# Two 64-row products per pair, padded with zeros to 128 rows

## The chip, the cores and the metric

The kernel runs on one core of one Trainium2 chip. The metric is device time in microseconds (us), as the median of several runs. The core's engines run side by side, each through its own instruction stream in order: TensorE (PE; its weight loads are listed as PEld) does matrix products into PSUM, VectorE (DVE), ScalarE (ACT) and GpSimd (POOL) do elementwise work, and SyncE (SP) issues DMAs, as ScalarE does for the weights.

## The reference

The model is a trunk of two layers over 1024 positions of width 1024, each followed by a SwiGLU block. Layer 0 mixes by spatial gating and pooling. Layer 1 is an RWKV-7 time mix, and of that this part matters here:

```python
wlog = -jax.nn.softplus(-(w0 + jnp.tanh(xw @ w1) @ w2).astype(f32)) - 0.5
...
a = jax.nn.sigmoid(a0 + (xa @ a1) @ a2)
g = jax.nn.sigmoid(xg @ g1) @ g2
...
k = k * (1 + (a - 1) * k_a)
...
decay = heads(jnp.exp(-jnp.exp(wlog)))
y = wkv7_scan(rh, decay, kh, vh, -kk, kk * ah)
```

The decay and the learning rate `a` each come from a product of rank 64: first 1024 to 64 (`w1`, `a1`), then 64 to 1024 (`w2`, `a2`). The gate has rank 160.

## The kernel before

Everything is held transposed, 128 features on the partitions and positions along the free dimension, in two halves of 512 positions. Products are made precise by splitting each float32 operand into a rounded part (hi) and the rest (lo) and adding three products: hi by hi, hi by lo, lo by hi (`mm3`, lines 343 to 346). Weights come by DMA in tiles of 128x1024 (`load_at`, line 108), and are split by ScalarE (line 145) and DVE (line 146) just ahead of their use.

For the two low-rank products of decay and learning rate the rank is 64, and the kernel uses the other 64 partitions for the lo part of the weights. The tiles `w2[0]` and `w2[1]` hold 128 rows: one half has the hi part of the 64 weight rows, the other half the lo part (`stack`, line 148; for decay the lo part is in rows 64 to 127, for the learning rate in rows 0 to 63). In `lowrank` (line 824) the tiles `tw` and `ta` get the hi part of the inner vectors twice, in both halves (line 840), so that one product of 128 rows gives hi by hi and lo by hi at once. The lo parts of the inner vectors share one tile, `twlo`: that of decay in rows 0 to 63, that of the learning rate in rows 64 to 127 (line 842). They meet only the hi half of the weights, in a second product of 64 rows:

```python
for z, w, x, r in ((zw, w2[0], twa[0], rows[0]), (za, w2[1], twa[1], rows[1])):
    pe.matmul(z, w[:, ms], x, start=True, stop=False)
    pe.matmul(z, w[r, ms], twlo[r], start=False, stop=True)
```

This stands at lines 998 to 1000 of `project`, which runs once for each half. Its order is: the gate's second product for 8 blocks of 128 features (lines 919 to 927; it reads the tiles `ghi`, `glo` and the 96-row `gst`, is evicted by ScalarE and sent to memory); then masks set by GpSimd (lines 932 to 937); then a loop over 8 pairs of heads. A pair does the k product (24 matmuls), the four low-rank matmuls above, tanh and sigmoid of their results (lines 1004 to 1007), the running sum of the decay (line 1011), its exponentials (lines 1015 and 1016), the r product (24 matmuls, with small products in between), the norms (lines 1024 to 1027 and 1037), and products of these elementwise (lines 1043 to 1060). The interaction of a pair (`interact`, line 941, with products at line 946) is emitted one pair later. After pairs 3 and 7 its results go through memory into the input of a triangular inversion (`invert`, lines 1106 to 1128), whose 31 steps run on DVE beside the pairs that follow. After the pairs comes the v product (line 1089).

The tiles `ghi`, `tw`, `ta` and `twlo` come from the pool `kp`, with one buffer for each tag.

Except where it is written out by hand, the order of instructions on each engine is made by a planner: it simulates the engines with estimated durations and picks by priority, which is mostly the order in which the program was written, among what it takes to be ready. A tile that takes over a buffer waits for all readers of the tile that had it.

Of the kernel before, what the change touches and what calls it, by code (L numbers as in the profile page):

```python
# [9 lines left out]
F32 = mybir.dt.float32  # L10
F32R = mybir.dt.float32r
AF = mybir.ActivationFunctionType
# [4 lines left out]
P = 128  # L17
# [3 lines left out]
HT = 512  # L21
# [17 lines left out]
def tile_trunk(  # L39
# [8 lines left out]
    act, dve, pool, pe, sp = nc.scalar, nc.vector, nc.gpsimd, nc.tensor, nc.sync  # L48
    x = x.flatten_outer_dims()
# [19 lines left out]
    def open_pool(**kw):  # L69
        es = ExitStack()  # L70
        pl = es.enter_context(tc.tile_pool(reuse_waits="tile", **kw))
        return pl if kw["name"].startswith("wp") else Lines(pl), es
# [60 lines left out]
    def take(key):  # L133
        i = pos[0]
        assert plan[i][0] == key, (plan[i][0], key)
        pos[0] += 1
        split_at(i)
        load_at(i + 1)
        if i + 1 in raws:
            load_at(i + 2)  # L140
        split_at(i + 1)
        return ready.pop(i)
# [189 lines left out]
    def auxt():  # L332
        return pst("aux")
# [234 lines left out]
    for m in ORD_Z:  # L568
# [4 lines left out]
        for h in range(2):  # L573
# [15 lines left out]
            s, w, base = zp, 1, 0  # L589
            while w < win:  # L590
# [4 lines left out]
                s, base, w = n, b0, 2 * w  # L595
# [193 lines left out]
    rows = [slice(0, 64), slice(64, 128)]  # L789
# [110 lines left out]
    def project(h, hn1, kp, ring, keep, before_v):  # L900
# [3 lines left out]
        def tmp(tag, bufs=1, shape=None, dt=F32):  # L904
            if early.get(tag):
                return early[tag].pop(0)
            return ep.tile(shape or [P, HT], dt, tag=tag, bufs=bufs, name=tag)
# [7 lines left out]
        w2 = tmp("w2", 1, [P, D], F32R), tmp("a2", 1, [P, D], F32R)  # L915
# [3 lines left out]
        for m in range(KT):  # L919
            ms = slice(m * P, (m + 1) * P)  # L920
# [6 lines left out]
                sp.dma_start(g_d[h][rows[m % 2], m // 2 * 2 + r, :], t[rows[r]])  # L927
        for n in range(2):
            take(("wa2", n, h))
        twa, twlo = (keep["tw"], keep["ta"]), keep["twlo"]  # L930
        smask = tmp("smask", 1, [P, 256])
        pool.memset(smask, 1.0)
        pool.memset(c64(smask)[:, :, 0:1], 0.0)
# [51 lines left out]
        for p in range(KT):  # L985
            ms = slice(p * P, (p + 1) * P)
# [8 lines left out]
            act.activation(kt, o, AF.Copy)  # L995

            zw, za = auxt(), auxt()
            for z, w, x, r in ((zw, w2[0], twa[0], rows[0]), (za, w2[1], twa[1], rows[1])):
                pe.matmul(z, w[:, ms], x, start=True, stop=False)
                pe.matmul(z, w[r, ms], twlo[r], start=False, stop=True)  # L1000
            if prev is not None:
                late(*prev)
            sg, av = tmp("sg", 2), tmp("av", 2)
# [31 lines left out]
            for j in range(4):  # L1035
                for r in range(2):
                    pe.matmul(
                        rb[rows[r], j * P : (j + 1) * P], bc(rn[:, 2 * j + r : 2 * j + r + 1], [P, 64]), ident,
                        start=True, stop=True,
# [457 lines left out]
    kp, kp_es = open_pool(name="keep0", bufs=1, side="right")  # L1497
    ring, ring_es = open_pool(name="ring0", bufs=1, side="right")
    f, f_es = open_pool(name="ffn0b", bufs=1, side="right")
    parts, keep = project_gate(0, hn1, kp, xlp, ring)  # L1500
# [14 lines left out]
    nxt = {}  # L1515
    ps_es = open_psum("psp0", PROJ)
    project(0, hn1, kp, ring, keep, early("n0", "act1", xlp_es))
    for e in (ring_es, kp_es, np_es):
        e.close()
# [15 lines left out]
    kp, kp_es = open_pool(name="keep1", bufs=1, side="right")  # L1535
# [6 lines left out]
    parts, keep = project_gate(1, hn1, kp, nxt["a"], ring)  # L1542
# [19 lines left out]
    for e in (f_es, y_es, hb_es, ps_es):  # L1562
        e.close()
    ps_es = open_psum("psp1", PROJ)
    project(1, hn1, kp, ring, keep, early("n1", "act2", nxt["a_es"]))
    for e in (ring_es, kp_es, np_es):
        e.close()
# [56 lines left out]
```

## Time and profile before

| | |
|---|---|
| median of 3 runs | 2528.8 us (2524.71 to 2532.28) |
| profiled execution | 2522.66 us, span 2520.9 us |
| mean granted TensorE clock | 0.983 |
| idle time of TensorE at line 1000 | 9.5 us over 32 matmuls, put down to issue |
| DVE lines 1117 and 1122, the inversion | from 825.7 us (first half) |
| SBUF-to-memory and weight traffic | 310.69 MB, mean 123 GB/s |

In the rows of the profile "L1000" is a line of the kernel, "aux<-twlo,w" is output and inputs by the program's names, "64\*128 64x512" is a stationary operand of 64 rows by 128 columns and a moving one of 64 rows by 512, and an arrow at the end names what ended the idle time before. The listed ends of matmuls are modelled and overlap; their starts are what to read.

### The profile page before, as it was taken

Reading aid. Unit: us, or ns where it says so; the run is one execution under the profiler, and the core shown is the slowest. Engines: PE = TensorE matmul, PEld = TensorE weight load, DVE = VectorE, ACT = ScalarE, POOL = GpSimd, SP = SyncE. Lnnn points to the kernel's source line nnn. Section 1 sums busy time; section 2 is a strip of 40 time slices with the busy share of each in tenths; the row PEclk is TensorE's granted clock in tenths of the full one; section 3 lists DMA queues with packets and bytes.
Section 4 is the critical chain, followed back from the end, with each engine's and each line's share of the span. In section 5 each row is a group of like instructions: output and inputs, shape, how many; then the busy total and the mean of one; then the engine's idle time right before and its main releaser. Section 6 shows DMA issues by size and latency. Waiting matters only on the chain.

```text
span 2520.9 us, 37945 instructions
## 1 busy us (share of the span) xinstructions
PE 2432.2 (96%) x15735; PEld 1983.2 (79%) x15735; DVE 1401.8 (56%) x2118; ACT 890.7 (35%) x1335; POOL 299.8 (12%) x298
## 2 busy tenths in 40 slices
PE   8999999999989998999999989899999999999998
PEld 6888888888767786788877667787888878888887
DVE  5445634444865873555457855964654445434443
ACT  6233322222544432333234643433333224323223
POOL 0200000000323410111001222401211000100001
PEclk9999999999999998999999999999999999999999
DMA  5113433323255478433334355585653332423331
GB/s 175 48 59 92 142 109 116 101 92 112 88 156 134 123 204 203 136 113 102 112 118 138 111 179 133 132 230 159 167 150 110 100 107 77 150 88 119 94 92 59
DMA packets 434956, 310.69 MB, mean 123 GB/s; under 512 B 93216, under 2 KB 395424, under 8 KB 433760
## 3 DMA queue, kind: packets, MB, share of 16 engines
q10 hardware_dynamic: 297280, 210.53, 27.9%
q1 hardware_dynamic: 137504, 97.75, 13.7%
q8 instruction: 123, 2.02, 0.3%
q14 instruction: 49, 0.40, 0.0%
HBM read 254.68 MB, written 53.54 MB: 122 GB/s over the span
## 4 chain that ended last, share of the span: by engine, by line
PE 74%; DVE 13%; DMA 7%; issue 3%; ACT 2%; POOL 1%; SPq 0%; ACTq 0%; DVEq 0%; POOLq 0%
PE mm L344 21%; PE mm L345 21%; PE mm L346 20%; PE sm L1168 4%; DVE wlo L146 2%; DMA raw<-in_ffn_w_up_dram 2%; DVE it L1117 1%; DVE mix L887 1%; DVE xi L1122 1%; DMA iat<-at_d 1%; PE yp L1168 1%; DMA raw<-in_ffn_w_down_dram 1%; PE mm L510 1%; PE mm L511 1%; ACT whi L145 1%
## 5 line engine op out<-in xcount | busy, mean ns | idle before, releaser
L344 PE MATMUL mm<-ahi,whi 128*128 128x512 f32 x1952 | 766.9, 394 | 5.1 <-DVE h L423 4.0
L345 PE MATMUL mm<-alo,whi 128*128 128x512 f32 x1952 | 769.1, 394 | 1.6 <-DVE alo L146 1.6
L346 PE MATMUL mm<-ahi,wlo 128*128 128x512 f32 x1952 | 766.5, 393 | 2.6 <-DVE wlo L146 2.6
L145 ACT ACTIVATE whi<-raw 128x1024 fp32r<-128x1024 f32 x288 | 304.3, 1058 | 768.1 <-PE mm L345 608.5
L146 DVE TENSOR_TENSOR wlo<-raw,whi 128x1024 fp32r<-128x1024 f32 x288 | 362.0, 1257 | 309.8 <-ACT whi L145 301.5
L344 PEld LDWEIGHTS mm<-ahi,whi 128*128 128x128 f32 x1952 | 367.9, 189 | 87.2 <-issue 4.5
L346 PEld LDWEIGHTS mm<-ahi,wlo 128*128 128x128 f32 x1952 | 368.2, 189 | 82.3 <-DVE wlo L146 3.4
L345 PEld LDWEIGHTS mm<-alo,whi 128*128 128x128 f32 x1952 | 368.2, 189 | 82.1 <-issue 3.7
L345 PE MATMUL mm<-hidlo,wdhi 128*128 128x512 f32 x624 | 246.6, 395 | 1.3 <-DVE hidlo L672 1.2
L344 PE MATMUL mm<-hidhi,wdhi 128*128 128x512 f32 x624 | 239.8, 394 | 6.6 <-ACT hidhi L671 5.2
L346 PE MATMUL mm<-hidhi,wdlo 128*128 128x512 f32 x624 | 245.5, 393 | 0.0
L423 DVE TENSOR_TENSOR h<-h,mm 128x512 f32<-128x512 f32 x192 | 129.2, 684 | 149.9 <-PE mm L346 149.1
L145 ACT ACTIVATE wdhi<-raw 128x1024 fp32r<-128x1024 f32 x82 | 86.6, 1059 | 254.9 <-DMA raw<-in_ffn_w_down_dram 150.8
L146 DVE TENSOR_TENSOR wdlo<-raw,wdhi 128x1024 fp32r<-128x1024 f32 x82 | 100.4, 1225 | 111.3 <-ACT wdhi L145 105.5
L668 DVE TENSOR_TENSOR sg<-sg,mm 128x512 f32<-128x512 f32 x88 | 60.2, 685 | 165.3 <-PE mm L346 164.9
L344 PEld LDWEIGHTS mm<-hidhi,wdhi 128*128 128x128 f32 x624 | 117.2, 188 | 35.2 <-ACT hidhi L671 7.4
L345 PEld LDWEIGHTS mm<-hidlo,wdhi 128*128 128x128 f32 x624 | 118.2, 189 | 27.9 <-DVE hidlo L672 3.2
L346 PEld LDWEIGHTS mm<-hidhi,wdlo 128*128 128x128 f32 x624 | 118.2, 189 | 24.6 <-issue 0.2
L423 DVE TENSOR_TENSOR hA<-hA,mm 128x512 f32<-128x512 f32 x72 | 48.7, 685 | 77.0 <-PE mm L346 77.0
L349 POOL TENSOR_TENSOR nrs<-nrs,small 128x4 f32<-128x4 f32 x8 | 10.0, 1246 | 625.4 <-DVE nrs L371 625.4
L344 PE MATMUL mm<-xhi,whi 128*128 128x512 f32 (+1 forms) x160 | 66.0, 412 | 4.2 <-ACT k L925 4.2
L672 DVE TENSOR_TENSOR hidlo<-sg,hidhi 128x512 fp32r<-128x512 f32 x88 | 64.5, 733 | 3.8 <-ACT hidhi L671 3.7
(300 smaller groups left out, 2952.1 us busy)
## 6 DMA issues: line engine op xcount, KB each, us to landing
raw<-in_ffn_w_gate_dram ACTq DMA_DIRECT2D x88, 512.0 KB
raw<-in_ffn_w_up_dram ACTq DMA_DIRECT2D x88, 512.0 KB
raw<-in_ffn_w_down_dram ACTq DMA_DIRECT2D x88, 512.0 KB
raw<-in_ab_w_in_dram ACTq DMA_DIRECT2D x16, 512.0 KB
raw<-in_ab_w_out_dram ACTq DMA_DIRECT2D x16, 512.0 KB
raw<-in_rwkv_w_k_dram ACTq DMA_DIRECT2D x16, 512.0 KB
raw<-in_rwkv_w_r_dram ACTq DMA_DIRECT2D x16, 512.0 KB
ar_d<-ar SPq DMA_DIRECT2D x16, 512.0 KB
```

Source lines behind the costliest of these rows:

```text
L145: act.activation(hi, src, AF.Copy)
L146: (eng or dve).tensor_tensor(out=lo, in0=src, in1=hi.bitcast(F32), op=ALU.subtract)
L344: pe.matmul(o, whi, xhi, start=first, stop=False)
L345: pe.matmul(o, whi, xlo, start=False, stop=False)
L346: pe.matmul(o, wlo, xhi, start=False, stop=last)
L423: dve.tensor_tensor(out=H[h][:, m, :], in0=H[h][:, m, :], in1=o, op=ALU.add)
L510: pe.matmul(ops[j], xhi[:, k, sl], whi[:, kk], start=(k == 0), stop=False)
L511: pe.matmul(ops[j], xhi[:, k, sl], wlo[:, kk], start=False, stop=False)
L668: dve.tensor_tensor(out=s, in0=s, in1=o, op=ALU.mult)
L672: dve.tensor_tensor(out=lo, in0=s, in1=hi.bitcast(F32), op=ALU.subtract)
L887: dve.scalar_tensor_tensor(out=t, in0=hn1[:, k, 0:HT], scalar=col(c), in1=t, op0=ALU.mult, op1=ALU.add)
L1168: i = f(*args, **kw)
```

## The change

The tile `twlo` keeps the lo part of decay in rows 0 to 63 and gets zeros in rows 64 to 127. A new tile, `talo`, takes over the buffer of `ghi`; ScalarE copies the lo part of the learning rate into its rows 64 to 127, and GpSimd sets its rows 0 to 63 to zero. The second product of each pair is then made over all 128 rows, with the full weight tile. The zero rows of the moving operand meet the lo half of the weights, so the result is the same.

```diff
         for n in range(2):
             take(("wa2", n, h))
-        twa, twlo = (keep["tw"], keep["ta"]), keep["twlo"]
+
+        twlo, talo = keep["twlo"], kp.tile([P, HT], F32R, tag="ghi", name="talo")
+        act.activation(talo[rows[1]], twlo[rows[1]].bitcast(F32), AF.Copy)
+        pool.memset(talo[rows[0]].bitcast(F32), 0.0)
+        pool.memset(twlo[rows[1]].bitcast(F32), 0.0)
+        twa, low = (keep["tw"], keep["ta"]), (twlo, talo)
...
             zw, za = auxt(), auxt()
-            for z, w, x, r in ((zw, w2[0], twa[0], rows[0]), (za, w2[1], twa[1], rows[1])):
+            for z, w, x, xl in ((zw, w2[0], twa[0], low[0]), (za, w2[1], twa[1], low[1])):
                 pe.matmul(z, w[:, ms], x, start=True, stop=False)
-                pe.matmul(z, w[r, ms], twlo[r], start=False, stop=True)
+                pe.matmul(z, w[:, ms], xl, start=False, stop=True)
```

## The prediction

> **What bounds the kernel now.** I read the page first, then TensorE's timeline around the products that the change touches, then the busy time by stage, and last the waits.
>
> ```profile
> span 2520.9 us, 37945 instructions
> ...
> PE 2432.2 (96%) x15735; PEld 1983.2 (79%) x15735; DVE 1401.8 (56%) x2118; ACT 890.7 (35%) x1335; POOL 299.8 (12%) x298
> ...
> PE 74%; DVE 13%; DMA 7%; issue 3%; ACT 2%; POOL 1%; SPq 0%; ACTq 0%; DVEq 0%; POOLq 0%
> ```
>
> TensorE is busy for 96% of the span and carries 74% of the chain that ended last. Time taken out of its stream is worth something wherever no other engine holds the next step. The stream must be read by starts, though: durations of matmuls overlap, so what one of them really costs is the distance from its start to the start of the next. The edit touches lines 999 and 1000. This is the timeline of TensorE around pair 3 of the first half (start, duration, engine, line):
>
> ```profile
> 790.63 0.39 PE L999 MATMUL aux<-tw,w 128*128 128x512 f32 x1
> 790.95 0.50 PE L1000 MATMUL aux<-twlo,w 64*128 64x512 f32 x1
> 791.38 0.49 PE L999 MATMUL aux<-ta,a 128*128 128x512 f32 x1
> 791.80 0.49 PE L1000 MATMUL aux<-twlo,a 64*128 64x512 f32 x1
> 792.23 0.50 PE L344 MATMUL mm<-ahi,whi 128*128 128x512 f32 x1
> 792.57 0.40 PE L345 MATMUL mm<-alo,whi 128*128 128x512 f32 x1
> 792.81 0.40 PE L346 MATMUL mm<-ahi,wlo 128*128 128x512 f32 x1
> ```
>
> Outside the block a product with 512 columns takes 0.24 us from start to start (792.57 to 792.81), or 0.23 in the rows further down. Inside it the distances are 0.32, 0.43, 0.42, 0.43 and 0.34 us. So five matmuls, the last of which is an ordinary one, take 792.57 - 790.63 = 1.94 us, where five at 0.23 us would take 1.15. The surplus is 0.79 us for a pair, or 0.40 us for each of its two 64-row products, split between the way in and the way out. The last pair of the second half looks the same:
>
> ```profile
> 1603.09 0.39 PE L999 MATMUL aux<-tw,w 128*128 128x512 f32 x1
> ...
> 1605.03 0.40 PE L345 MATMUL mm<-alo,whi 128*128 128x512 f32 x1
> ```
>
> Again 1605.03 - 1603.09 = 1.94 us. The view of the tile twlo (durations in ns as least/median/most) shows that these products are few and alike:
>
> ```profile
> L1000 PE MATMUL aux<-twlo,w x16: 497/498/792, 726.8 to 1603.4; 64*128 64x512 f32 x16
> L1000 PEld LDWEIGHTS aux<-twlo,a x16: 182/183/183, 732.0 to 1604.3; 64*128 64x128 f32 x16
> L1000 PE MATMUL aux<-twlo,a x16: 491/491/498, 732.0 to 1604.3; 64*128 64x512 f32 x16
> ```
>
> There are 32 of them, two for each of 8 pairs in each of 2 halves. At 0.40 us each the whole surplus is 12.8 us, or 0.5% of the span. That is the ceiling of the direct gain.
>
> **Is it the 64 rows?** The timeline holds a product with a third number of rows, the 96-row one of the gate:
>
> ```profile
> 731.24 0.39 PE L346 MATMUL mm<-ghi,wlo 128*128 128x512 f32 x1
> 731.47 0.40 PE L923 MATMUL mm<-gst,whi 96*128 96x512 f32 x1
> 731.70 0.40 PE L999 MATMUL aux<-ta,a 128*128 128x512 f32 x1
> ```
>
> It fits into the stream at 0.23 us on either side, although it too has fewer rows than the products around it, another stationary operand, and closes an accumulation of its own. So neither a smaller count of rows by itself nor the close of a group costs anything here; going from the 128-row form to the 64-row form and back does. A product padded to 128 rows has the shape of its neighbours, and I take its cost to be theirs, 0.23 us. The Trainium skill, page "TensorEngine Tiling (Array Packing)", section "Key Properties", has a rule that would give this sum: a change of the tiling mode drains the array. Its page "TensorE: Matmul & The Clock Gate", section "Why this matters for your kernels", has one that speaks against the change: a single product of 32 rows takes the same time as one of 128, so rows would be free and zeros would buy nothing. The rows above (0.43 against 0.23 us) agree with the first; the second comes back as a rival.
>
> **What passes to the end.** The pairs do not all lie under the same bound. Busy time in two stretches of each half (start:end and length, then PE, PEld, DVE, ACT, POOL, then the granted clock):
>
> ```profile
> 757.00:824.00 67.00, 67.00 (x474) 52.60 (x474) 35.67 (x48) 26.68 (x39) 22.24 (x24) 1.00 0.55 141
> 824.00:880.00 56.00, 50.87 (x333) 39.08 (x331) 52.29 (x95) 26.71 (x40) 26.18 (x21) 0.94 0.44 111
> 1499.00:1564.00 65.00, 65.00 (x453) 51.23 (x454) 34.69 (x47) 25.98 (x38) 22.21 (x24) 1.00 0.57 146
> 1564.00:1622.00 58.00, 52.45 (x342) 40.95 (x342) 53.15 (x96) 26.68 (x40) 26.33 (x21) 0.94 0.42 108
> ```
>
> In the first stretch of each half, pairs 1 to 4, TensorE never idles and the clock is 1.00, with DVE at 35.67 of 67 us. There each 0.79 us passes in full: 8 pairs x 0.79 = 6.3 us.
>
> In the second stretch, pairs 5 to 7, DVE is busy for 52.29 of 56 us, because the inversion (lines 1117 and 1122) has joined it, and TensorE is the one that waits:
>
> ```profile
> PE aux L946 <- DVE bk L1055: 7.4, 5, 3.4
> PE aux L999 <- DVE w L153: 6.5, 2, 4.6
> ...
> PE mm L344 <- ACT k L925: 4.2, 2, 2.1
> ```
>
> The stretch begins when the inversion gets its input after a round trip by DMA, for which DVE stands idle:
>
> ```profile
> 825.69 0.19 DVE L1117 TENSOR_TENSOR it<-iat,xi 128x31 f32<-128x31 f32 x1 [6.49 <-DMA iat<-at_d]
> ```
>
> That input comes from pair 3's interaction product, which follows the block of pair 4, so it comes forward by what pairs 1 to 4 save. What pairs 5 to 7 save themselves may only make the waits on DVE longer. Their 6 pairs x 0.79 = 4.7 us are worth between 0 and 4.7 us. DVE at 93% (52.29 of 56) speaks for little, TensorE at 91% (50.87 of 56) for much; I take half, 2.4 us.
>
> **What is added.** For each half: one ScalarE copy of 64x512, and two GpSimd fills of 64x512. The nearest rows, of the view of line 840 and of the groups by form:
>
> ```profile
> L840 ACT ACTIVATE tw<-low x4: 613/623/632, 667.2 to 1408.8; 64x512 fp32r<-64x512 f32 x4
> ```
>
> ```profile
> L1142 POOL MEMSET state_d<- 128x512 f32 x1 | 0.5, 524 | 0.0
> ```
>
> The copy is 0.62 us and a fill 0.52 us, by the row with as many columns, so 0.62 us of ScalarE and 1.05 us of GpSimd in each half, on engines busy for 35% and 12%. The padded product reads the full 128x128 weight tile, which the product before it loads anyway; the weights need no new instruction.
>
> More important is an ordering. The new tile takes the single buffer of ghi, so the copy has to wait for the last gate product that reads ghi. The copy reads the rows of twlo that are then set to zero, so both low products of pair 0 wait for this chain, that of decay too. In the trace of before they ran early, at 726.80 and 732.03, as filler between gate products. Queued behind the copy on ScalarE are evictions, splits and the tanh of pair 0; behind the fills on GpSimd stand smask, ind2 and the inversion's first fill. These rows tell who would notice:
>
> ```profile
> 734.18 0.39 PE L923 MATMUL mm<-gst,whi 96*128 96x512 f32 x1
> ...
> 736.67 0.50 PE L344 MATMUL mm<-xhi,whi 128*128 128x512 f32 x1 [2.10 <-ACT k L925]
> ...
> 738.43 0.64 ACT L1015 ACTIVATE epx<-cum 128x512 f32<-128x512 f32 x1
> ...
> 749.50 0.69 DVE L1059 TENSOR_TENSOR ar<-mm,epx 128x512 f32<-128x512 f32 x1 [3.35 <-DMA raw<-in_rwkv_w_k_dram]
> ```
>
> The gate ends at 734.18 + 0.39 = 734.57; a copy and one fill later (1.14 us) it is 735.7, and TensorE now waits for ScalarE until 736.67. That 2.10 us of idle time covers the chain; were it gone, the chain would cost 1.1 us a half. Pair 0's exp at 738.43 has 11.1 us until its first use at 749.50, so a later sigmoid and scan are covered as well. The bounds for pair 0, both halves together: a gain of about 3 us, half of the 6.5 us for which TensorE waits for DVE w at its first product, if that one no longer stands ahead of the gate's (half, because no row tells how soon the gate's could start), and a loss of about 4 us, if 1.1 us of chain and 0.9 us of displaced filler (four products at 0.23) stand open in each half. The idle row lies nearest to nothing lost, so I take 0, and also for its own share of the surplus (32 - 28 = 4 products, 1.6 us), since it sits in a stretch where TensorE waits anyway.
>
> **The sum.** 6.3 + 2.4 + 0 = 8.7 us less. The profiled execution took 2522.66 us, of which 2520.9 are its span; by the sum the same execution would take 2514.0 us. It lies 6.1 us below the median of the runs, 2528.8; applied to the median, the forecast is 2520.1 us.
>
> **Rivals.** *The gain is given back on other engines.* The products get cheaper, but pairs 5 to 7 pass nothing on (2.4 us less gain) and pair 0 pays its 4 us: 6.3 - 4 = 2.3 us gained, 2526.5 us. For it speak DVE's 93% and the in-order wait of ScalarE just where the copy goes in; against it the 2.10 us of idle cover. The planner orders all instructions by its own estimate of when each is ready, and three more instructions a half can shift that order; this too falls in here.
>
> *Rows are free.* The surplus of 0.79 us belongs to something that padding doesn't touch, so nothing is saved, and the copy's 0.62 us stands open in each half: 2528.8 + 1.2 = 2530.0 us. This is also the case in which the change does not do what it says. For it stands that part of the surplus, the 0.32 us from 790.63 to 790.95, already follows a 128-row product; against it the 96-row product, which has everything but the 64-row form and costs 0.23 us. The Trainium skill's rule on a single small product, named above, would give this case; the trace bears it out badly.
>
> *Pair 0 comes late.* The planner, seeing that the low products of pair 0 must wait, may put them behind its k product and its r product, 24 matmuls each, 11 us together. Then they come not at 726.80 but at about 736.67 + 11.0 = 747.7, 20.9 us later, and the exp follows by as much: past the 11.1 us of slack by about 10 us, for which DVE would stand at line 1059 with the splits of the next weights queued behind it. Open in both halves, that is 20 us against 8.7 gained: 2540 us. It turns the result to the slow side from 8.2 us a half on ((8.7 + 7.6) / 2). Against it: the low product needs only the copy and a fill, and TensorE is idle at just that time.
>
> **How the numbers follow.** A measurement of this kernel can tell about 0.3%, 7.6 us, from no change. The forecast with its mechanism has 0.57, given back 0.30, rows free 0.05, pair 0 late 0.08. Faster by over 0.3% means below 2521.2; the forecast lies only 1.1 us beyond that line, so the chances are 0.57 faster, 0.35 the same (given back and rows free), 0.08 slower. The range starts at the ceiling with pair 0's gain, 2528.8 - 12.8 - 3 = 2513.0, and ends at 2529.0, just past no change; the late pair and the worst of rows free stay outside.
>
> **What would show it right or wrong.** The products of lines 999 and 1000 should both read 128x512, 16 for each operand, and stand 0.23 us apart, so that the block from the first to the second matmul behind it takes about 1.15 us instead of 1.94; if it still takes 1.9, rows are free. The stretch of pairs 1 to 4 should be shorter by about 3 us in each half, with TensorE still without idle time. In pairs 5 to 7 the wait on DVE bk should grow by less than 2.4 us a half; if by all of that, I put too much there. At the end of the gate, the wait for ScalarE should not exceed 2.1 us and no wait for GpSimd should appear on the first low product; if one of several us does, pair 0 was mispriced. Waits in the recurrence and in the dense stages should be as before; if they differ by several us, the order was laid anew and my sum is not the whole story.

## The result, and the profile after

The changed kernel takes 2514.06 us (median of 7 runs, 2508.43 to 2517.13), beside 2525.61 us for the kernel before in the same series (7 runs, 2522.41 to 2532.28). The ratio, which goes by the means of the runs, is 0.9947, with a 95% interval of 0.9933 to 0.9962: 13.4 us less, give or take 3.7. The two medians lie 11.6 us apart. The forecast was 8.7 us less, and 2520.1 us as a time; that time started from a median of 3 runs, 2528.8 us, which lies 3.2 us above the one of 7. The profiled execution took 2514.61 us, with a span of 2512.9 us.

The first thing to read is the block that the change touches. This is the changed kernel's TensorE timeline around pair 3 of the first half (start, duration); lines 999 and 1000 are now 1004 and 1005:

```profile
787.23 0.39 PE L1004 MATMUL aux<-tw,w 128*128 128x512 f32 x1
787.45 0.39 PE L1005 MATMUL aux<-twlo,w 128*128 128x512 f32 x1
787.68 0.39 PE L1004 MATMUL aux<-ta,a 128*128 128x512 f32 x1
787.91 0.39 PE L1005 MATMUL aux<-talo,a 128*128 128x512 f32 x1
788.13 0.39 PE L344 MATMUL mm<-ahi,whi 128*128 128x512 f32 x1
788.36 0.39 PE L345 MATMUL mm<-alo,whi 128*128 128x512 f32 x1
```

All starts are 0.22 or 0.23 us apart, and from the first matmul to the second one behind the block it is 788.36 - 787.23 = 1.13 us, where it was 1.94. The change does what it says, at a price per product that is the neighbours' own.

Next, the stages. The table is worked out from starts of matmuls in the two profiled executions. "Pair 0" runs from the third 96-row product of the gate to pair 1's first low-rank product; "pairs 1 to 4" from there to pair 5's; "pairs 5 to 7" from there to the last interaction product of pair 7; the other rows lie between these.

| stage, us | before | after | difference |
|---|---|---|---|
| pair 0, first half | 37.99 | 35.13 | -2.86 |
| pairs 1 to 4 | 65.34 | 62.53 | -2.81 |
| pairs 5 to 7 | 66.25 | 65.41 | -0.84 |
| between the halves | 573.3 | 570.0 | -3.3 |
| pair 0, second half | 34.95 | 32.37 | -2.58 |
| pairs 1 to 4 | 65.34 | 62.77 | -2.57 |
| pairs 5 to 7 | 66.64 | 67.74 | +1.10 |
| tail: from there to the last matmul | 881.6 | 887.1 | +5.5 |

One execution of each is not enough to trust single rows, so both were profiled again, as they are and with one small fill written twice (experiment 1), and the 96-row kernel of experiment 2, whose order is that of the changed one, counts with it. Averaged over three profiles on the side of the kernel before and four on that of the changed one, pair 0 gained 2.9 and 1.6 us, pairs 1 to 4 2.8 and 2.6, pairs 5 to 7 0.4 and then lost 0.9, the stretch between the halves gained 3.4, and the tail lost 3.9. Pairs 1 to 4 hardly vary (65.34 each time before, 62.52 to 62.85 after). Pair 0 of the second half does (32.37 to 35.69 after), and so does the tail: 881.6 to 886.7 before, 886.9 to 891.2 after.

Pairs 1 to 4 by engine (start:end and length, then busy us of PE, PEld, DVE, ACT, POOL, then the granted clock, the share of the DMA engines' time and GB/s), the kernel before and then the changed kernel, two halves each:

```profile
759.10:824.40 65.30, 65.30 (x456) 51.48 (x455) 34.69 (x47) 26.03 (x40) 22.24 (x24) 1.00 0.57 145
1498.90:1564.30 65.40, 65.40 (x457) 51.50 (x455) 34.69 (x47) 26.14 (x40) 22.21 (x24) 1.00 0.57 145
```

```profile
756.80:819.30 62.50, 62.01 (x457) 51.76 (x456) 34.70 (x47) 25.74 (x40) 22.23 (x24) 1.00 0.59 152
1487.10:1549.90 62.80, 62.07 (x457) 51.81 (x456) 34.70 (x47) 25.79 (x40) 22.23 (x24) 1.00 0.59 151
```

The same work on every engine, in less time; but PE is now idle for 0.5 and 0.7 us, where it had no idle time. The wait view of the first of these stretches names what is late next:

```profile
PE aux L1042 <- POOL rn L349: 0.5, 1, 0.5
```

That is one wait in pair 1 for the norms that GpSimd works on. From pair 2 on, the distance from pair to pair (first low-rank product to first low-rank product) is 16.03 us, before 16.89.

Pairs 5 to 7, before (the first two rows) and after:

```profile
824.40:890.70 66.30, 61.17 (x393) 47.51 (x391) 62.02 (x111) 29.62 (x44) 30.02 (x24) 0.90 0.48 128
1564.30:1630.90 66.60, 57.67 (x391) 45.19 (x391) 61.55 (x109) 29.55 (x44) 30.62 (x24) 0.95 0.47 125
```

```profile
819.30:884.70 65.40, 57.42 (x392) 46.70 (x391) 61.16 (x109) 29.36 (x44) 30.02 (x24) 0.92 0.48 127
1549.90:1617.60 67.70, 55.98 (x393) 46.44 (x391) 61.40 (x110) 29.31 (x44) 28.58 (x24) 0.93 0.47 125
```

DVE is busy for 62 us of 66 before and for 61 us of 65 to 68 after. PE's busy time falls by 3.8 and 1.7 us, and the stretch by 0.8 us in the first half, while it grows by 1.1 in the second. The granted clock moves the same way, up in the first half and down in the second. The waits of the changed kernel (over the whole span: total us, times, longest) that answer to those shown of before read:

```profile
PE aux L951 <- DVE bk L1060: 14.3, 6, 3.6
PE sm L1173 <- DVE gt L1220: 8.8, 3, 3.9
...
PE aux L1004 <- DVE w L153: 5.8, 2, 4.0
...
PE sm L1175 <- DMA bk<-bk_d: 4.1, 2, 3.4
...
PE aux L1005 <- ACT talo L932: 2.8, 2, 1.4
```

Of the kernel before, the two that the prediction does not show are:

```profile
PE sm L1168 <- DVE gt L1215: 10.8, 6, 4.1
...
PE sm L1170 <- DMA bk<-bk_d: 1.9, 1, 1.9
```

The wait for DVE bk grew from 7.4 to 14.3 us. Within pairs 5 to 7, over the three and four profiles, it grew by 1.8 us in the first half and 5.0 in the second. The idle time before the k product (4.2 us, twice 2.1) is gone from the list, and a wait of 1.4 us a half on the copy `talo` has come.

Last, pair 0. The changed kernel's timeline at the end of the gate:

```profile
733.39 0.39 PE L923 MATMUL mm<-gst,whi 96*128 96x512 f32 x1
735.22 0.47 PE L1005 MATMUL aux<-talo,a 128*128 128x512 f32 x1 [1.43 <-ACT talo L932]
735.75 0.50 PE L344 MATMUL mm<-xhi,whi 128*128 128x512 f32 x1
736.08 0.39 PE L345 MATMUL mm<-xlo,whi 128*128 128x512 f32 x1
736.31 0.40 PE L346 MATMUL mm<-xhi,wlo 128*128 128x512 f32 x1
...
737.92 0.39 PE L344 MATMUL mm<-xhi,whi 128*128 128x512 f32 x1
```

The low product of the learning rate now stands inside the idle time that was there anyway. The k product behind it runs at 0.23 us a matmul. In the kernel before it did not:

```profile
737.27 0.63 PE L346 MATMUL mm<-xhi,wlo 128*128 128x512 f32 x1
737.70 0.63 PE L344 MATMUL mm<-xhi,whi 128*128 128x512 f32 x1
...
740.26 0.56 PE L344 MATMUL mm<-xhi,whi 128*128 128x512 f32 x1
```

From 737.27 to 740.26 there are seven steps of 0.43 us where 0.23 would do, 1.4 us more than at full speed. The stretch from pair 0's first to pair 1's first low-rank product, before (first two rows) and after, shows the granted clock of it:

```profile
726.10:759.10 33.00, 30.90 (x131) 23.72 (x131) 10.48 (x11) 13.26 (x19) 3.10 (x4) 0.88 0.58 167
1466.20:1498.90 32.70, 30.55 (x130) 23.72 (x130) 10.61 (x11) 15.10 (x23) 3.81 (x7) 0.90 0.58 178
```

```profile
726.20:756.80 30.60, 29.07 (x131) 23.17 (x131) 10.52 (x11) 13.90 (x20) 4.51 (x6) 0.92 0.62 181
1457.00:1487.10 30.10, 28.63 (x131) 22.62 (x131) 10.56 (x11) 15.78 (x24) 4.75 (x8) 0.94 0.63 192
```

At 0.88 of 33.0 us, 4.0 us are lost to the clock, at 0.92 of 30.6 us 2.4: 1.5 us less, and as much in the second half (3.3 against 1.8). With the surplus of 0.79 us that makes 2.3 of the 2.4 and 2.6 us by which this stretch became shorter. Over the three and four profiles the account holds as well: the stretch became 2.9 and 1.6 us shorter, with 2.0 and 1.1 us less lost to the clock. In the profiles of all kernels of this document, half-speed time of some 3.4 us falls on pair 0's k and r products in 19 of 20 halves where pair 0 has 64-row products, and in 1 of 16 where it has none. That one, with 5.7 us, is the second half of the changed kernel's second profile, whose pair 0 took the 35.69 us.

### The profile page after: what moved, and what is told of

The parts are those of the page before. It is cut to its first block, busy times and chain, and to the rows that moved or that the text cites. A ratio compares the mean times of both kernels' runs of the same rounds, so it can differ in the third digit from the quotient of the medians.

```text
span 2512.9 us, 37956 instructions
## 1 busy us (share of the span) xinstructions
PE 2421.1 (96%) x15735; PEld 1987.5 (79%) x15735; DVE 1401.4 (56%) x2118; ACT 890.2 (35%) x1337; POOL 302.4 (12%) x302
## 3 DMA queue, kind: packets, MB, share of 16 engines
q1 hardware_dynamic: 137504, 97.75, 13.7%
## 4 chain that ended last, share of the span: by engine, by line
PE 74%; DVE 12%; DMA 7%; issue 3%; ACT 2%; POOL 1%; SPq 1%; ACTq 0%; DVEq 0%; POOLq 0%
PE mm L345 21%; PE mm L344 21%; PE mm L346 21%; PE sm L1173 5%; DVE wlo L146 2%; DVE it L1122 1%; DVE xi L1127 1%; PE yp L1173 1%; DVE mix L887 1%; DMA raw<-in_ffn_w_up_dram 1%; DMA iat<-at_d 1%; DMA raw<-n_d 1%; DVE alo L146 1%; ACT whi L145 1%; PE mm L510 1%
```

## The experiments

The theory behind the first runs was the prediction's own: the 64-row form costs 0.4 us more a product among 128-row ones, DVE takes what pairs 5 to 7 save, and pair 0 is neutral. Rivals: rows matter and not the form; the new order, not the padding, made the gain; the gain is one draw among many orders that the planner could have made. All kernels here compute the whole reference.

**1. Is it the order by itself?** Three kernels are the kernel before, the changed kernel and the one of experiment 4, each with one fill of the mask written twice. That was meant to have the planner lay out the instructions in another order.

```diff
         pool.memset(c64(smask)[:, :, 0:1], 0.0)
+        pool.memset(c64(smask)[:, :, 0:1], 0.0)
```

Expected of the kernel before with it: 

> The kernel before with one fill of GpSimd (128 rows, 4 columns, 0.10 us) written twice, in each half, and nothing else. It asks how much the planner's order alone is worth. Theory (any edit lays the order behind the pairs anew, and that moves the time by several us either way): pairs 1 to 5 at 65.34 us as before, but the stretch behind the last pair's interaction of the second half, 881.6 and 884.9 us in two profiles of the kernel before, comes out 3 to 10 us different, and the ratio lies anywhere from 0.997 to 1.004. Rival (the order matters little, the give-back in the padded kernels comes from the padding): stretch 881 to 886 us, ratio 1.000 within 0.001.

Of the changed kernel: 

> The changed kernel with the same neutral edit as in the neutral run: one small fill written twice, which lays the planner's order behind the pairs anew. Theory (the padding is worth 5.4 us in pairs 1 to 5 for certain, pair 0's new place 3 to 5 us, and the order behind decides the rest by several us either way): pairs 1 to 5 at 62.5 to 62.8 us, pair 0's stretch at 32 to 36 us, but the time anywhere from 0.993 to 0.999. Rival (the gain of the changed kernel is its own, whatever the order): 0.9947 within 0.0015.

Of experiment 4's kernel: 

> Padding for pairs 1 to 7 alone, with the same neutral edit. It had gained 6 us in the pairs and nothing in the end. Theory (the order behind took it back): with another order a part of the gain shows, ratio 0.996 to 0.999, from a shorter stretch behind the last interaction than 891 us. Rival (a gain in the pairs without pair 0 is given back in any order, because the stages behind wait for something else): ratio 1.000 within 0.0015 again.

Measured, as ratios to the kernel before: 0.9999 (0.9988 to 1.0011), 0.9949 (0.9934 to 0.9964) and 1.0002 (0.9991 to 1.0013). Each kernel keeps its time. But the edit did not do what it was meant to: in the traces of each kernel with it and without it, VectorE and ScalarE have the same instructions in the same order, GpSimd has too but for the two added fills, and TensorE's lists differ in 6 or 7 of 15735 entries, where two profiles of one kernel differ in 1 to 11. So these runs are repeats. They show that 0.53% is no chance of single runs, and that experiment 4's kernel comes back with no gain; what another order would be worth they do not say, and neither the theory nor the rivals of their expectations were put to the test. The changed kernel's own order differs from that of the kernel before in 204 entries of TensorE, 51 of VectorE and 34 to 36 of ScalarE. Second profiles of the three kernels without the edit, on another occasion, gave 2525.67, 2513.88 and 2520.91 us for single executions.

Expected of these: 

> The kernel before once more, for a second profile. In its first profile the stretch from the first product of the last pair to the last matmul took 909.4 us in the second half, and that between the halves 604.1 us; in the changed kernel these were 917.8 and 600.8. Theory (the stretch behind the pairs varies from execution to execution by several us, the same program in the same order): the long stretch comes out somewhere between 909 and 920 us, while the pairs themselves repeat within 1 us. Rival (the stretch belongs to the program's order): 909.4 within 2 us again, and the changed kernel gives 8 us back there for good.

> The changed kernel once more, for a second profile. Theory (variation between executions): the long stretch, 917.8 us at first, moves by several us, the stretches of the pairs (30.5 us from pair 0 to pair 1, 99.5 us from pair 1 to pair 7) repeat within 1 us. Rival (order): 917.8 within 2 us.

> Padding for pairs 1 to 7 alone, once more. Its pairs gained 6.8 us over both halves and its time nothing; the long stretch took 923.2 us in its profile, 13.8 more than in the first profile of the kernel before. Theory (variation): it comes out shorter by several us. Rival (its order costs there): 923 within 2 us.

Measured, for the stretch that these texts speak of (from the last pair's first product to the last matmul): 913.4, 917.6 and 920.8 us. Of 909.4, 917.8 and 923.2 two moved by 4.0 and 2.4 us and one by 0.2, so single profiles vary by some us there, and the kernel before still has the shortest stretch.

**2. Rows or form?** Two kernels. In one the low product of decay is given 96 rows in place of 128, with everything else as changed:

```diff
-            for z, w, x, xl in ((zw, w2[0], twa[0], low[0]), (za, w2[1], twa[1], low[1])):
+            for z, w, x, xl, r in ((zw, w2[0], twa[0], low[0], slice(0, 96)), (za, w2[1], twa[1], low[1], slice(0, 128))):
                 pe.matmul(z, w[:, ms], x, start=True, stop=False)
-                pe.matmul(z, w[:, ms], xl, start=False, stop=True)
+                pe.matmul(z, w[r, ms], xl[r], start=False, stop=True)
```

> The changed kernel, but decay's second product reads only rows 0 to 95 (rows 64 to 95 are zeros); the learning rate's keeps 128 rows. Theory (the price is that of changing between the 128-row and the 64-row form): 96 rows keep the form of 128, so the block from the first low-rank product of a pair to the second matmul behind it stays at 1.13 to 1.16 us and the time equals the changed kernel's, ratio 0.9947 to the kernel before, within 0.003. Rival (the fewer rows, the dearer a product among 128-row ones): decay's product costs about 0.2 us more than 0.23, the block reads about 1.35 us, and some 3 us of the gain are lost, ratio 0.996.

Measured: 0.9957 (0.9942 to 0.9971), and in the timeline of pair 3:

```profile
786.90 0.39 PE L1004 MATMUL aux<-tw,w 128*128 128x512 f32 x1
787.12 0.40 PE L1005 MATMUL aux<-twlo,w 96*128 96x512 f32 x1
787.36 0.40 PE L1004 MATMUL aux<-ta,a 128*128 128x512 f32 x1
787.59 0.40 PE L1005 MATMUL aux<-talo,a 128*128 128x512 f32 x1
```

A 96-row product with the same operands takes 0.24 us to the next start, and the products ahead of it and behind it take 0.22 and 0.23. So the price does not grow with each row left out: 96 rows cost nothing, and 64 cost 0.4 us. It belongs to the 64-row form, as the theory had it.

The other takes the kernel before, without padding, and puts the two 64-row products side by side:

```diff
             for z, w, x, r in ((zw, w2[0], twa[0], rows[0]), (za, w2[1], twa[1], rows[1])):
                 pe.matmul(z, w[:, ms], x, start=True, stop=False)
+            for z, w, r in ((zw, w2[0], rows[0]), (za, w2[1], rows[1])):
                 pe.matmul(z, w[r, ms], twlo[r], start=False, stop=True)
```

> The kernel before, without padding, but with both 128-row products of a pair ahead of both 64-row products, so that pairs 1 to 7 change form twice instead of four times (pair 0 is kept by the planner as it was). Theory (a price for each change of form, about 0.2 us): the block of 1.94 us falls to about 1.5 us, 0.43 us less a pair; pairs 1 to 4 pass that on, 8 x 0.43 = 3.4 us, of pairs 5 to 7 about half as in the changed kernel: 4 to 5 us faster, ratio 0.998. If the two 64-row products, which lie in different halves of the rows, also run side by side, another 0.2 us a pair: ratio 0.9975. Rival (a price for each 64-row product, wherever it stands): the block stays at 1.94 us and the ratio is 1.000.

Measured: 0.9993 (0.9982 to 1.0004). The block did get shorter:

```profile
791.29 0.39 PE L999 MATMUL aux<-tw,w 128*128 128x512 f32 x1
791.52 0.39 PE L999 MATMUL aux<-ta,a 128*128 128x512 f32 x1
791.84 0.50 PE L1001 MATMUL aux<-twlo,w 64*128 64x512 f32 x1
791.84 0.50 PE L1001 MATMUL aux<-twlo,a 64*128 64x512 f32 x1
792.27 0.50 PE L344 MATMUL mm<-ahi,whi 128*128 128x512 f32 x1
792.61 0.40 PE L345 MATMUL mm<-alo,whi 128*128 128x512 f32 x1
```

From the first to the second matmul behind: 792.61 - 791.29 = 1.32 us. The two products on different halves of the rows start in the same instant, and the two together pay about 0.4 us and not 0.8 (0.32 on the way in, 0.43 and 0.34 on the way out, less three steps of 0.23). That fits a price for each change of form; since the two ran side by side, a price for each product, paid by both at the same time, is not ruled out. Pairs 1 to 4 gained 2.2 us a half, from 65.34 to 63.15 and 63.16, and the tail, 882.5 us, stayed as in the kernel before. About as much, 4.2 us, shows in the profile (the last matmul starts at 2508.3 us, before at 2512.5). Over all runs it is 4.5 us at most by the interval, and may be nothing, where the theory had 0.998 or 0.9975. That a gain in these pairs need not be seen in the end opened the question of where it goes.

**3. The order alone, with 64-row products.** The copy, both fills and the wait of the changed kernel stay, and the second products go back to 64 rows, so that pair 0 has its new order and nothing is padded in the products. (Elsewhere the planner's order differs from the changed kernel's in 138 entries of TensorE, 36 of VectorE and 22 of ScalarE.)

```diff
...
-                pe.matmul(z, w[:, ms], xl, start=False, stop=True)
+                pe.matmul(z, w[r, ms], xl[r], start=False, stop=True)
```

> The changed kernel with its copy, its two fills and its wait for the gate's tile, but with products of 64 rows out of the new tiles, as before. It separates the padding from the new order of pair 0. Padding theory: pairs 1 to 7 take 1.94 us a block again, so all of the gain but pair 0's is gone; for pair 0, whose stretch from its first product to pair 1's shrank by 2.5 us in each half, a part must come from the order (the learning rate's low product moves behind the gate): between 1 and 4 us in both halves together, ratio 0.999. Rival (most of the gain comes from the new order, and the padded products are worth little): ratio 0.996 or lower.

Measured: 1.0012 (0.9998 to 1.0025). So the new place of pair 0's low products brings nothing by itself, and from here to the 96-row kernel of the same series, which has the changed kernel's order, it is 13.7 us by the medians (2528.07 to 2514.41). Pair 0 took 37.33 and 35.02 us here, 0.9 and 0.3 less than the mean of the kernel before and 2.1 and 1.3 more than that of the changed kernel. The wait on the copy is about the same size in the first half (in the second it is 2.2 us, in the changed kernel 1.4), but the half-speed stretch is still there, if a little later:

```profile
735.55 0.50 PE L1005 MATMUL aux<-talo,a 64*128 64x512 f32 x1 [1.34 <-ACT talo L932]
736.17 0.50 PE L344 MATMUL mm<-xhi,whi 128*128 128x512 f32 x1
...
737.77 0.63 PE L344 MATMUL mm<-xhi,whi 128*128 128x512 f32 x1
738.20 0.63 PE L345 MATMUL mm<-xlo,whi 128*128 128x512 f32 x1
```

**4. Padding in pairs 1 to 7 alone.** Pair 0 keeps its 64-row products, early as before, and the copy and the fills come behind it:

```diff
...
-                pe.matmul(z, w[:, ms], xl, start=False, stop=True)
+                pe.matmul(z, w[:, ms] if p else w[r, ms], xl, start=False, stop=True)
+            if p == 0:
+                talo = kp.tile([P, HT], F32R, tag="ghi", name="talo")
...
+                low = twlo, talo
```

> Padding for pairs 1 to 7 alone: pair 0 multiplies 64 rows out of the old tile, early and between the gate's products as before, and the copy and the fills come behind it. Theory (pairs 1 to 7 are worth about 8 us, pair 0 about 5): blocks of pairs 1 to 7 at 1.15 us, pair 0's stretch back at about 33 us in each half with the 2.1 us wait for ScalarE and the half clock behind it; 8 us faster than before, ratio 0.997, and about 5 us slower than the changed kernel. Rival (pair 0 adds nothing in the long run, since the stages behind it give it back): ratio 0.9947 as for the changed kernel.

Measured: 0.9999 (0.9985 to 1.0013). Pairs 1 to 4 took 62.54 and 62.79 us, so they have all their gain; pair 0 has none (38.75 and 35.73), with the old clock and an idle time of 2.9 us ahead of the k product, before 2.1. Neither 0.997 nor 0.9947 came out. The stretch from pair 0's first to pair 1's first low-rank product:

```profile
726.20:759.90 33.70, 30.82 (x130) 23.73 (x130) 10.46 (x11) 14.06 (x20) 4.13 (x6) 0.88 0.55 163
1460.00:1493.40 33.40, 30.51 (x130) 23.66 (x130) 10.57 (x11) 15.96 (x24) 4.82 (x8) 0.90 0.57 175
```

What pairs 1 to 4 gained was given back behind the pairs: the tail took 892.2, 890.0 and 895.3 us in the three profiles of this kernel and its copy with the doubled fill, against 881.6 to 886.7 in three of the kernel before. Experiment 3's kernel, with 64-row products, has the same long tail, 892.5 us. So a long tail needs no padded products. Summed over the wait view of the tail, PE's idle time is 15.8 us on average in the three profiles of experiment 4's kernel against 11.7 in the kernel before and 13.6 in the changed one; and half-clock time in the tail is 18 to 22 us against 13.7 and 15, of which half is lost. Together that is 7.0 of the 8.1 us by which the tail of this kernel is longer than the mean of the kernel before, and 2.6 of the 3.9 us of the changed kernel. It says what the time is, not why the waits grow.

**5. Pair 0 with the low products behind the gate.** The changed kernel, with all four low-rank products of pair 0 held until the last product of the gate, so that they fill the idle time:

```diff
-            pe.matmul(o, g2b[:96, ms], keep["gst"][:96], start=False, stop=True)
+            gated = pe.matmul(o, g2b[:96, ms], keep["gst"][:96], start=False, stop=True).ins
...
-                pe.matmul(z, w[:, ms], x, start=True, stop=False)
-                pe.matmul(z, w[:, ms], xl, start=False, stop=True)
+                with tc.issue_after(gated):
+                    pe.matmul(z, w[:, ms], x, start=True, stop=False)
+                    pe.matmul(z, w[:, ms], xl, start=False, stop=True)
```

> The changed kernel with the four low-rank products of pair 0 told to follow the last product of the gate, so that none of them stands ahead of gate products in TensorE's stream. If the first product's wait for DVE (4.0 and 1.9 us in the changed kernel) holds up the gate, the gate's products start sooner and pair 0's stretch shrinks by up to 2 us in each half: ratio 0.993. Rival (the gate is held by the evictions and the weights' splits, so that the wait only moves): pair 0's stretch within 0.5 us of the changed kernel's 30.5 us, ratio as the changed kernel's, 0.9947.

Measured: 0.9955 (0.994 to 0.9971). Pair 0 became shorter again, to 33.47 and 31.89 us, and the whole time did not: the tail took 890.6 us. That is 1.8 us a half below the mean of the changed kernel, and nothing of it can be measured at the end.

**6. Does DVE hold pairs 5 to 7?** The first attempt asked for fewer steps of the inversion between the pairs (3 for 5), in the changed kernel, the kernel before, and experiment 5's kernel:

```diff
-RATIO, AHEAD, INV, FINE = 3.0, 450, 5, 1
+RATIO, AHEAD, INV, FINE = 3.0, 450, 3, 1
```

> The changed kernel with 3 inversion steps instead of 5 at each of the slots that the pairs and the v product give to the inversion. Theory (pairs 5 to 7 pass on nothing because DVE holds them, with the inversion queued ahead of their elementwise steps): fewer steps there, TensorE waits less for DVE at line 951, and the stretch from pair 5 to the last interaction, 65.4 to 68.2 us in the changed kernel, falls by 2 us or more in each half; ratio 0.992 if the rest stays. Rival (other work holds DVE there): the stretch stays within 1 us and the inversion only ends later.

> The kernel before with 3 inversion steps instead of 5. Theory (DVE holds pairs 5 to 7): without padding TensorE's own time for them is longer by 0.8 us a pair, so that it and the changed kernel with 3 steps differ in the stretch from pair 5 to the last interaction by about 2 us, where with 5 steps they differed by 0.5 us or less; the stretch itself falls from 66 to 67 us. Rival: no difference between the two, as with 5 steps.

> A version to beat both: the changed kernel with pair 0's low-rank products behind the gate and 3 inversion steps. If the gains of the two add: stretch from the gate's first block to pair 1 at 32 to 33.5 us, from pair 5 to the last interaction 64 us or less, ratio 0.991 to 0.993. If the order behind takes them back: ratio 0.995.

Measured: 0.9987 (0.9975 to 0.9998), 1.0026 (1.0013 to 1.004) and 0.9986 (0.9973 to 1.0). The planner put 26 or 27 steps into the stretch all the same, which took 65.8 to 67.9 us as before, so this said nothing about DVE. The changed kernel took 8.9 us less than the kernel before here too. Both are slower than without the edit, by about 10 and 7 us by the ratios, so what stands where in the order is worth several us.

The second attempt takes the inversion out of the stretch: its steps wait for the last elementwise step of pair 7, in the kernel before and in the changed one.

```diff
-                if next(inv[0], "end") == "end":
+                with tc.issue_after(held):
+                    step = next(inv[0], "end")
+                if step == "end":
...
-            invert_on(INV)
...
-            dve.scalar_tensor_tensor(out=kt, in0=o, scalar=col(C_RK + p), in1=kt, op0=ALU.mult, op1=ALU.mult)
+            held = dve.scalar_tensor_tensor(out=kt, in0=o, scalar=col(C_RK + p), in1=kt, op0=ALU.mult, op1=ALU.mult).ins
```

> The kernel before with VectorE's inversion steps all held back behind the last elementwise step of pair 7, so that nothing of the inversion stands between VectorE's pair steps. It is the base for the next kernel. Theory (VectorE's queue sets the pace of pairs 5 to 7): the stretch from pair 5's first low-rank product to pair 7's last interaction product, 66.3 and 66.6 us before, shortens, to below 65 us. The whole time is of no interest: the inversion's steps come later, and it may grow by some us per half. Rival (the pairs' own chain through VectorE or the transfers set the pace): the stretch stays within 0.7 us of 66.3.

> The changed kernel with the same edit. Theory (the padding's gain in pairs 5 to 7 was swallowed by VectorE's queue): with the inversion out of the way this stretch is shorter than the one of the kernel before with the same edit by about 2.4 us in each half (three pairs by the surplus of 0.8 us per pair), as it is in pairs 1 to 4. Rival: it is shorter by 0.5 us or less, as with the inversion in place, and then something else holds these pairs.

Measured: 1.0087 (1.007 to 1.0104) and 1.0023 (1.0012 to 1.0034), 2550.63 and 2532.48 us. The stretch, kernel before with the edit first:

```profile
824.00:881.00 57.00, 54.91 (x393) 43.50 (x391) 41.92 (x54) 30.02 (x44) 27.49 (x24) 0.99 0.53 140
1570.90:1627.00 56.10, 54.55 (x393) 43.10 (x392) 41.57 (x54) 30.04 (x44) 27.54 (x24) 1.00 0.54 140
```

```profile
820.20:875.10 54.90, 52.12 (x391) 43.32 (x391) 41.51 (x54) 30.01 (x44) 27.55 (x24) 1.00 0.55 143
1550.60:1605.00 54.40, 52.11 (x393) 43.32 (x391) 41.53 (x54) 29.99 (x44) 27.57 (x24) 1.00 0.56 146
```

Without the inversion's 20 us DVE is busy for 42 of 57 us, the clock is 0.99 to 1.00, and the stretch is 9 to 11 us shorter in the kernel before already. Now the padding passes: 2.0 us in the first half and 1.6 in the second (56.94 to 54.92, 56.03 to 54.42 by starts), where three pairs' surplus is 2.4. From pair 5 to 6 and from 6 to 7 it is 15.93 us against 16.79, so the 0.86 us of a pair passes there in full. Without the inversion DVE has less to do and the clock does not drop, and these runs do not tell the two apart. And here the tail is the same in both kernels, 915.9 and 916.0 us: nothing is given back behind the pairs, and the padding is worth 18.2 us between the medians, more than the 13.4 of the change as it is (8.9 us of it lie between the halves in these two profiles, a stretch that varies by 6 us from profile to profile of one kernel). The two kernels are slower than without the edit, since the inversion then stands in the open.

## Where the prediction was right and where it was wrong

The direction and the mechanism were right: the 64-row form costs, padding removes it, and the block went from 1.94 to 1.13 us where 1.15 was forecast. That refutes "rows are free", and by experiment 2 rows left out cost nothing as long as there are 96 (0.22 to 0.24 us). The size was wrong: 13.4 us (give or take 3.7) were measured where the sum has 8.7. The step that failed is the term of pair 0, put at 0, where its two stretches gained 4.6 us. A second term was wrong the other way: pairs 5 to 7, put at 2.4 us, gave nothing.

The page "TensorE: Matmul & The Clock Gate" of the Trainium skill, section "Why this matters for your kernels", says that a product of 32 rows alone takes as long as one of 128. No run here has 32 rows. For 96 rows the trace agrees with rows being free, for 64 rows among 128-row products it differs (0.43 us from the 64-row product's start to the next, against 0.23), and the measurement decides. The Trainium skill's page "TensorEngine Tiling (Array Packing)", section "Key Properties", has a change of mode drain the array. Experiment 2's pair of 64-row products, which pays 0.4 us and not 0.8, fits that and does not prove it.

By terms:

- **Pairs 1 to 4, 6.3 us forecast: 5.4 measured** (2.81 and 2.57). From pair 2 on each pair gave 0.86 us, a little more than 0.79; in pair 1 a wait of 0.5 and 0.7 us for GpSimd's norms came in its place. The prediction held that each 0.79 passes in full since TensorE never idles there; it did not look for what is late next by less than one surplus.
- **Pairs 5 to 7, "I take half, 2.4": nothing measured** (0.84 gained, 1.10 lost; over all profiles 0.4 gained, 0.9 lost). DVE's inversion as the reason stands: with it gone, 3.6 us pass (experiment 6). Its 93% should have been taken at its word, not halved by TensorE's 91%: the busiest engine of the stretch was the one waited for, and what TensorE saved turned into its wait. The prediction's own test says as much, "if by all of that, I put too much there": the wait on DVE bk grew by 6.9 us in all, more than the whole 4.7 that padding saved, most of it in the second half. Of the three waits that the prediction lists for these pairs only this one stands there; those on DVE w and ACT k stand in pair 0. The second wait of pairs 5 to 7 is that on GpSimd's norms, 5.2 us.
- **Pair 0, "I take 0": a gain of 5.4 us in these two profiles, 4.6 on average.** This is the step that failed, and its size is about that of the 4.7 us which the forecast lacked (13.4 - 8.7), though the interval of 3.7 us makes that agreement loose. The low product moved into the idle time as forecast, and the wait for ScalarE stayed within 2.1 us, with none for GpSimd on the first low product. But two things were left out. The surplus of 0.79 us a half was written off because "TensorE waits anyway", while the stretch has a busy k product and r product behind the wait. And the granted clock was not looked at: 0.88 and 0.90 of full speed before, 0.92 and 0.94 after, worth 1.5 us a half. The bound for a gain, about 3 us, was too tight.
- **What lies behind the pairs, taken as unchanged: 3.4 us gained between the halves and 3.9 lost in the tail.** The waits of the recurrence moved by 2 us each (on DVE gt from 10.8 to 8.8, on the DMA of bk from 1.9 to 4.1), so by the prediction's test the sum was not the whole story there. The two cancel nearly, which was luck.

The average sum is -4.6 - 5.4 + 0.5 - 3.4 + 3.9 = -9.0 us. That is near the 8.7 forecast by luck: 4.6 us too little in pair 0 stand against 3.8 too much in pairs 1 to 7. All runs together show 13.4 us. The 4 to 5 us between the two are not placed; part of it is that the profiled execution of the kernel before lies 2.9 us below its median (2522.66 against 2525.61) and that of the changed kernel 0.5 us above its own. The "ceiling" of 12.8 us counted no clock, and experiments 3 and 6 have 13.7 and 18.2 us; in the two profiles of experiment 6 half-clock time is 119.5 and 109.2 us, a difference worth 5.1 us of work.

Is the rest the order? No two kernels here differ by the padding alone and have one order. Four comparisons, each with orders of its own, point the same way: 13.4, 13.7 (experiment 3), 8.9 and 18.2 us (experiment 6). In a fifth, experiment 4, seven of eight pairs are padded and nothing is left at the end. Pairs 1 to 4 tell it without the order: they took 65.34 us in every kernel with the block of before, which experiment 3's and the unpadded ones of experiment 6 have too, and 62.5 to 62.9 us in every one with padded products. So it is shown that padding shortens TensorE's stream, by 0.8 us a pair where nothing else is waited for; how much of the 13.4 us it owes to the order that came with it is not.

Of the rivals, "the gain is given back" was nearer to life than the result tells: experiment 4's kernel saves what pairs 1 to 4 have to give and ends at no change, by a tail that is 8 us longer, and experiment 3's has that tail without saving anything. "Pair 0 comes late" did not happen. The low product of decay did slide behind the k product, from 726.80 to 741.32, and pair 0's exp came 7.6 us later, at 746.03. Its first use on DVE waited 1.2 us for ScalarE, and TensorE waited for none of it.

Three things stay open. Why the tail's waits and half-clock time depend on the order within the pairs: experiment 1 shows that it comes back with the same kernel, experiment 3 that it needs no padded products, experiment 6 that the difference between the two tails is gone with the inversion held back. Why the half-speed stretch in pair 0 disappears when the new order and the padding come together and not with the new order alone (padding alone was not run there): idle times of 1.34 and 1.43 us ahead of it are almost alike. And the 3.4 us between the halves, which lie within what single profiles of one kernel differ by there (567.7 to 573.3 before).

## What to carry to other kernels

Price a matmul by the distance between starts, next to its neighbours, and by its form: one product on half of the rows between full ones cost 0.4 us more than a full one here, so zeros were cheaper than fewer rows. Then ask stage by stage who is waited for: a saving on TensorE passed in full where TensorE was the only engine without idle time, was stopped at half a microsecond by the next one in line, and vanished where DVE was at 93%. And read the granted clock of each stage beside its busy time: pair 0 gained 1.5 us a half by the clock, and 0.79 by the products themselves. Last, before an edit is used to vary the order of a planned kernel, compare the two orders; a fill written twice left it as it was.

## What the runs showed of the hardware

Two products of 64 rows on different halves of the rows start at the same time (791.84 twice), so a pair of them pays about 0.4 us for the way in and out together, and not twice that. A product of 96 rows costs what a full one does (0.24 us against 0.23). The granted clock drops to half in stretches of 3.4 us or multiples of it (in the kernel before from 723.54 for 6.83 us and from 737.20 for 3.41 us, behind waits of up to 4.6 us for DVE w and of 2.1 us for ACT k), and each 3.4 us of it costs 1.7 us of work. In all it was 72 to 89 us per execution, on average 82 in the kernel before and 80 in the changed one, so most of the clock that pair 0 gained was spent in other stages.
